# Norms by one-column sums, a power and a spreading product, with later deadlines for the recurrence and the heads

## The chip, the cores and the metric

The program runs on one core of a Trainium2 chip. The metric is the device time of one execution in microseconds. A core has five engines that run their own queues of instructions: TensorE (PE in the profile; PEld is its weight load, which can run beside a product), VectorE (DVE), ScalarE (ACT), GpSimd (POOL) and SyncE (SP, which here issues the DMA transfers). Semaphores tie the queues together; within one queue instructions start in order.

## The reference

A residual block over 2048 tokens of 1024 features, in fp32. RMS norms stand in five places of it: before the input projection, on the recurrent branch, before the feed-forward part and at the end (the retention heads have a norm of their own, per head).

```python
def rms_norm(x, gain):
    xf = x.astype(jnp.float32)
    y = xf * lax.rsqrt(jnp.mean(xf * xf, axis=-1, keepdims=True) + NORM_EPS)
    return (y * gain.astype(jnp.float32)).astype(x.dtype)
...
    u = rms_norm(h, norm1_gain[l])
    proj = u @ w_in[l].astype(dt)
    x_lru, g_lru, q, k, v, g_ret = jnp.split(proj, SPLITS, axis=-1)
    xc = causal_depthwise_conv(x_lru, lru_conv_w[l], lru_conv_b[l])
    hl = rg_lru(xc, ...)
    y_lru = rms_norm(hl.astype(dt) * jax.nn.gelu(g_lru), lru_norm_gain[l])
    o = head_group_norm(retention_chunkwise(qh, kh, vh), ret_norm_gain[l])
    y_ret = o.reshape(bsz, slen, D_RET) * jax.nn.silu(g_ret)
    h = h + jnp.concatenate([y_lru, y_ret], axis=-1) @ w_out[l].astype(dt)
    u = rms_norm(h, norm2_gain[l])
    up = causal_depthwise_conv(u @ ffn_up_w[l].astype(dt), ffn_conv_w[l], ffn_conv_b[l])
    a_branch, v_branch = jnp.split(up, 2, axis=-1)
    h = h + (jax.nn.gelu(a_branch) * v_branch) @ ffn_down_w[l].astype(dt)
return rms_norm(h, final_norm_gain)
```

## The kernel before

Activations lie transposed: features on the 128 partitions, tokens in columns, two groups of 1024 tokens (g is 0 or 1). [...]

**Products.** A projection works on blocks in a Strassen scheme: a unit of seven block products (`px`, `pe`, `py` and `pq` are their PSUM banks) makes what eight plain ones would. Each fp32 product is made of three of a reduced type: a block is cast into a high part (ACT, `wh` for weights and `bh` for activations), the rest is subtracted (DVE, `wl` and `bl`), and PE runs high by high, high by low and low by high. So a block product is twelve PE instructions 128x512 between whose operands ACT and DVE stand. `wv` is a half block of that kind, `s` a sum of two weight blocks `wa` and `wb`. There are 745 block products in the program: the input projection for both groups (A0, A1: products 0 to 171), the output projection (B0, B1), the up projection (24 units per group) and the down projection. Product numbers below count them in PE's order.

**Norms.** Where a norm is due (class `SumSq` and function `rstd`), ACT squares each 128x1024 tile, DVE adds the squares into `sqacc`, PE multiplies a half of `sqacc` by a matrix of ones (`mst`: every partition gets the sum), ACT takes the root of it with the mean and epsilon folded in, and DVE takes the reciprocal into `rb`, which `normed` multiplies in. That is done by the recurrence's norm (`LruGroup`), the norm behind the output projection (`NormGroup`) and the last one (`FinalGroup`; its `piece` does the last 1024 columns in pieces of 512, 256 and 256). Norm 1 sums over tokens on partitions instead: there the sums are a column `ms`, POOL raises it to the power -0.5 (`cst`), `diagonal` makes diagonal blocks `dg` of it on DVE, and PE spreads them over partitions with the matrix of ones (`pb`), which ACT copies into `rb`.

**What sets the order.** A planner (class `Flow`) emits all instructions, engine by engine, in the order in which they come in its own planned time. Pieces of work are generators; `yield t0 + 8` gives the rest of a piece the due tick `t0 + 8`, and a tick is one block product. Among instructions that could start, the one with the earliest due tick goes first. The planner's costs are methods `cost_pe`, `cost_v`, `cost_a` and `cost_p`. `LruOut` is the recurrence of one 128-feature tile: `first` makes convolution, gates (`pa`, `pg`), exponent, root and scan, `second` the gelu gate. `QkOut` and `VgOut` do rotation, transposes (`pt`), scores (`sc`) and outputs (`po`) of a head. Tiles come from 54 slots in SBUF; PSUM has three banks of the kind `sm` for all small products. The trace counts each product of fp32 operands (`mst`, `pb`, `pt`) as two PE instructions, the planner's order as one.

Every instruction of the program is recorded under one line of the source, that of the helper that calls the engine (L122), so the trace is read by tiles.

Of the kernel before, what the change touches and what calls it, by code (L numbers as in the profile page):

```python
# [25 lines left out]
F32 = mybir.dt.float32  # L26
# [22 lines left out]
SOON = 1.5  # L49
ISSUE = 0.45  # L50
# [50 lines left out]
class Engine:  # L101
# [30 lines left out]
    def cost_v(self, op, n, args, kw):  # L132
        if op == "tensor_tensor_scan":
            return 0.2 + 2.1e-3 * n
        if op in ("tensor_scalar", "tensor_copy", "memset"):
            return 0.15 + 0.535e-3 * n
        if op == "bn_stats":
            return 0.3
# [175 lines left out]
def hymba_block_kernel(ctx: ExitStack, tc: tile.TileContext, xh, xn, win, wout, wup, down, gates, vecs,  # L314
# [100 lines left out]
    eps = cp.tile([P, 1], F32, name="eps")  # L415
# [21 lines left out]
    def constants():  # L437
        yield v.memset(cst, -0.5)
        yield v.memset(eps, EPS)
# [119 lines left out]
    class Unit:  # L559
# [13 lines left out]
        def weights(self, t0):  # L573
# [3 lines left out]
            def first():  # L577
# [5 lines left out]
                fl.spawn(sums(), t0 - 5)  # L583
                yield t0 - 6
# [3 lines left out]
            def sums():  # L588
# [4 lines left out]
                yield t0 - 4  # L593
                self.w["s1"] = yield from split(s1, "w")
                self.there["s1"].on = True
                yield t0 - 2
# [7 lines left out]
                yield t0 + 2  # L604
# [7 lines left out]
            fl.spawn(first(), t0 - 8)  # L612
# [345 lines left out]
    def diagonal(rt, n):  # L958
        dg = yield Slot("dg")
        op = None  # L960
        for t in range(n):
            o = v.tensor_scalar(out=blk(dg, t), in0=idt, scalar1=rt[:, t:t + 1], scalar2=None, op0=ALU.mult)
            op = op + o if op else o
        yield op
        return dg

    def spread(rt, out):

        yield have["idt"]
        dg = yield from diagonal(rt, NCH)  # L970
        r = yield Slot("rb")
        for n in range(2):
            pb = yield Bank("sm", "pb")
            op = None
            for t in range(4):
                o = pe.matmul(blk(pb, t), ones, blk(dg, 4 * n + t), start=True, stop=True)
                op = op + o if op else o
            yield op
            yield a.copy(r[:, half(n)], pb)
            free(pb)  # L980
        free(dg)
        out.append(r)

    def rstd(ss, n, out):

        r = yield Slot("rb")
        for i in range(2):
            pm = yield Bank("sm", "mst")
            yield pe.matmul(pm, ones, ss.acc[:, half(i)], start=True, stop=True)
            yield a.activation(r[:, half(i)], pm, AF.Sqrt, scale=1.0 / n, bias=eps)  # L990
            free(pm)
            yield v.reciprocal(r[:, half(i)], r[:, half(i)])
        free(ss.acc)
        out.append(r)
# [31 lines left out]
    def norm1(g, start, due):  # L1026
# [4 lines left out]
        def one(t):  # L1031
# [6 lines left out]
            if left[0] == 0:  # L1038
                yield v.tensor_scalar(out=ms, in0=ms, scalar1=1.0 / D, scalar2=EPS, op0=ALU.mult, op1=ALU.add)
                yield p.tensor_tensor(out=ms, in0=ms, in1=cst.to_broadcast([P, NCH]), op=ALU.pow)  # L1040
                out = []
                yield from spread(ms, out)
                rb1[g] = out[0]
# [5 lines left out]
    class LruOut(PlainOut):  # L1049
# [6 lines left out]
        def second(self):  # L1056
            t0 = self.unit.t0
            yield t0 + 12
# [578 lines left out]
```

## Time and profile before

| | us |
|---|---|
| median of 3 runs | 2222.85 (2222.07 to 2223.22) |
| the profiled execution | 2223.36 |
| its span in the profile | 2221.6 |
| PE busy | 2165.6 |
| DVE busy | 1805.9 |
| ACT busy | 1237.3 |
| POOL busy | 25.9 |

Busy times are sums over the whole span; what an engine did in one stage is read from the trace in order of time. An idle time in brackets behind a PE instruction is time in which PE had nothing to run, and the name behind the arrow is the instruction that ended last of those that it waited for.

### The profile page before, as it was taken

To read this page: it belongs to the slowest core of one execution; us is meant where nothing else is said; L and a number is where in the kernel's file an instruction comes from. 1 tells how busy PE (TensorE), PEld (TensorE's weight loads), DVE (VectorE), ACT (ScalarE), POOL (GpSimd) and SP (SyncE) were. 2 spreads that over 40 slices of the span, in tenths; PEclk is the share of its full clock that TensorE was granted. 3 is DMA by queue.
4 is the path that set the end of the run, shared out by engine and by line. 5 is a ranking of instruction groups with operands and counts; after the bars stand their busy time and mean duration, and the time that the engine had idled before them with its cause. 6 is when DMAs were issued, how large, how long until landed. Compare 5 with 4: busy or idle time off the path is not lost.

```text
span 2221.6 us, 26370 instructions
## 1 busy us (share of the span) xinstructions
PE 2165.6 (97%) x9772; PEld 1776.6 (80%) x9772; DVE 1805.9 (81%) x2250; ACT 1237.3 (56%) x1773; POOL 25.9 (1%) x22
## 2 busy tenths in 40 slices
PE   9989989999999999999999999999999999999996
PEld 7868867888788887888888878888888788878885
DVE  7999788777675788989788897878788887798776
ACT  6665565556633166666666866666667444344341
POOL 0000000000000000000000000000000000000000
PEclk9999999999999999999999999999999999999998
DMA  8965355133656953444233532323236577589762
GB/s 324 372 212 200 111 201 166 60 96 116 207 183 236 330 214 127 175 139 173 93 105 128 209 118 83 122 90 114 90 108 227 225 283 288 220 304 344 256 226 76
DMA packets 140528, 408.32 MB, mean 184 GB/s; under 512 B 15728, under 2 KB 20208, under 8 KB 140400
## 3 DMA queue, kind: packets, MB, share of 16 engines
q1 hardware_dynamic: 140400, 406.65, 51.7%
q8 instruction: 76, 1.25, 0.2%
q14 instruction: 52, 0.43, 0.1%
HBM read 273.16 MB, written 125.04 MB: 179 GB/s over the span
## 4 chain that ended last, share of the span: by engine, by line
PE 89%; DVE 6%; ACT 2%; DMA 1%; issue 1%; SPq 0%; DVEq 0%; ACTq 0%
PE py L122 32%; PE px L122 21%; PE pe L122 20%; PE pq L122 12%; PE po L122 1%; DVE rb L122 1%; DVE res L122 1%; DVE o L122 1%; PE pk L122 1%; PE sc L122 1%; DVE bl L122 1%; PE pt L122 1%; DVE wl L122 1%; PE pa L122 1%; PE pg L122 0%
## 5 line engine op out<-in xcount | busy, mean ns | idle before, releaser
L122 PE MATMUL py<-bh,wh 128*128 128x512 f32 x728 | 289.9, 398 | 12.8 <-ACT wh L122 8.8
L122 PE MATMUL py<-bh,wl 128*128 128x512 f32 x728 | 287.8, 395 | 9.0 <-DVE wl L122 9.0
L122 PE MATMUL pe<-bh,wh 128*128 128x512 f32 x728 | 287.4, 395 | 1.6 <-DVE o L122 1.6
L122 PE MATMUL py<-bl,wh 128*128 128x512 f32 x728 | 286.7, 394 | 0.0
L122 PE MATMUL pe<-bl,wh 128*128 128x512 f32 x728 | 283.7, 390 | 2.2 <-DVE bl L122 2.1
L122 PE MATMUL px<-bh,wh 128*128 128x512 f32 x728 | 285.3, 392 | 0.0
L122 PE MATMUL pe<-bh,wl 128*128 128x512 f32 x728 | 283.6, 390 | 0.1
L122 PE MATMUL px<-bh,wl 128*128 128x512 f32 x728 | 283.5, 389 | 0.0
L122 PE MATMUL px<-bl,wh 128*128 128x512 f32 x728 | 283.3, 389 | 0.0
L122 ACT CAST wh<-s 128x1024 fp32r<-128x1024 f32 x182 | 190.4, 1046 | 162.9 <-DVE s L122 151.5
L122 DVE TENSOR_TENSOR wl<-s,wh 128x1024 fp32r<-128x1024 f32 x182 | 222.1, 1220 | 67.6 <-ACT wh L122 67.2
L122 DVE SCALAR_TENSOR_TENSOR c<-o,vec,c 128x1022 f32<-128x1022 f32 x192 | 245.3, 1279 | 13.8 <-ACT c L122 8.3
L122 PE MATMUL py<-bh,wv 128*128 128x512 f32 x728 | 242.5, 394 | 2.4 <-ACT o L122 1.6
L122 ACT COPY o<-py 128x512 f32<-128x512 f32 x204 | 119.9, 588 | 206.0 <-PE py L122 205.3
L122 ACT CAST bh<-raw 128x1024 fp32r<-128x1024 f32 x158 | 162.6, 1050 | 58.0 <-DMA raw<-g 15.0
L122 DVE TENSOR_TENSOR bl<-raw,bh 128x1024 fp32r<-128x1024 f32 x158 | 189.1, 1218 | 3.6 <-ACT bh L122 2.5
L122 PEld LDWEIGHTS py<-bh,wh 128*128 128x128 f32 x728 | 139.3, 191 | 44.9 <-ACT wh L122 10.9
L122 ACT ACTIVATE c<-o,vec 128x1024 f32<-128x1024 f32 x96 | 119.6, 1246 | 97.3 <-DVE o L122 95.9
L122 PEld LDWEIGHTS py<-bh,wl 128*128 128x128 f32 x728 | 138.7, 191 | 41.3 <-DVE wl L122 12.2
L122 PE MATMUL pq<-bh,wh 128*128 128x512 f32 (+1 forms) x432 | 168.5, 390 | 1.2 <-ACT bh L122 0.7
L122 PE MATMUL pq<-bl,wh 128*128 128x512 f32 (+1 forms) x432 | 165.2, 382 | 0.7 <-DVE bl L122 0.7
L122 PE MATMUL pq<-bh,wl 128*128 128x512 f32 (+1 forms) x432 | 165.0, 382 | 0.5 <-DVE wl L122 0.5
(136 smaller groups left out, 3822.5 us busy)
## 6 DMA issues: line engine op xcount, KB each, us to landing
wa<-in_dram SPq DMA_DIRECT2D x91, 512.0 KB, 4.0
wb<-in_dram SPq DMA_DIRECT2D x91, 512.0 KB, 4.8
h<-res SPq DMA_DIRECT2D x56, 512.0 KB, 3.5
g_T<-t SPq DMA_DIRECT2D x96, 256.0 KB, 2.4
raw<-g_T SPq DMA_DIRECT2D x48, 512.0 KB, 6.6
res<-h SPq DMA_DIRECT2D x48, 512.0 KB, 6.3
g<-c SPq DMA_DIRECT2D x76, 256.0 KB, 3.1
raw<-g SPq DMA_DIRECT2D x38, 512.0 KB, 6.7
```

The lines of the kernel that those rows point to most:

```text
L122: return Op(self.name, lambda: fn(*args, **kw), us, writes, reads, func=func)
```

## The change

`rstd` no longer multiplies by a matrix of ones. Each 128-column block of `sqacc` becomes the weights of a product with one column of ones, so that eight products leave the sums as a column of eight values per partition; DVE scales them and adds epsilon, POOL raises them to the power -0.5, and `spread` makes from each column a repeated column as weights, by which the identity is multiplied; ACT copies the two banks into `rb`. Norm 1 uses the same `spread` and loses its diagonal blocks. The planner gets a cost for reciprocals, of which a small one is left. `CH` puts off the due ticks of the recurrence and of the heads by 6; `WB`, for the weights, is 0.

```diff
+WB = 0
+CH = 6
...
+        if op == "reciprocal":
+            return 0.15 + 6.1e-3 * n
...
-        yield v.memset(eps, EPS)
...
-    def diagonal(rt, n):
-        dg = yield Slot("dg")
+    def spread(rt, c0, c1, r):
+
+        yield have["idt"]
+        for b in range(c0, c1, Q):
+            w = min(Q, c1 - b)
+            pb = yield Bank("sm", "pb")
+            op = None
+            for t in range(w // P):
+                k = (b - c0) // P + t
+                o = pe.matmul(blk(pb, t), rt[:, k:k + 1].to_broadcast([P, P]), idt, start=True, stop=True)
+                op = op + o if op else o
+            yield op
+            yield a.copy(r[:, b - c0:b - c0 + w], pb[:, 0:w])
+            free(pb)
+
+    def rstd(acc, n, r, c0=0, c1=HT):
+
+        nb = (c1 - c0) // P
+        rt = sp.tile([P, NCH], F32, tag="ms", name="ms")[:, 0:nb]
+        pm = yield Bank("sm", "mst")
         op = None
-        for t in range(n):
-            o = v.tensor_scalar(out=blk(dg, t), in0=idt, scalar1=rt[:, t:t + 1], scalar2=None, op0=ALU.mult)
+        for t in range(nb):
+            o = pe.matmul(pm[:, t:t + 1], acc[:, c0 + t * P:c0 + (t + 1) * P], ones[:, 0:1], start=True, stop=True)
             op = op + o if op else o
         yield op
-        return dg
-
-    def spread(rt, out):
-
-        yield have["idt"]
-        dg = yield from diagonal(rt, NCH)
-        r = yield Slot("rb")
-        for n in range(2):
-            pb = yield Bank("sm", "pb")
-            op = None
-            for t in range(4):
-                o = pe.matmul(blk(pb, t), ones, blk(dg, 4 * n + t), start=True, stop=True)
-                op = op + o if op else o
-            yield op
-            yield a.copy(r[:, half(n)], pb)
-            free(pb)
-        free(dg)
-        out.append(r)
-
-    def rstd(ss, n, out):
-
-        r = yield Slot("rb")
-        for i in range(2):
-            pm = yield Bank("sm", "mst")
-            yield pe.matmul(pm, ones, ss.acc[:, half(i)], start=True, stop=True)
-            yield a.activation(r[:, half(i)], pm, AF.Sqrt, scale=1.0 / n, bias=eps)
-            free(pm)
-            yield v.reciprocal(r[:, half(i)], r[:, half(i)])
-        free(ss.acc)
-        out.append(r)
+        yield v.tensor_scalar(out=rt, in0=pm[:, 0:nb], scalar1=1.0 / n, scalar2=EPS, op0=ALU.mult, op1=ALU.add)
+        free(pm)
+        yield p.tensor_tensor(out=rt, in0=rt, in1=cst.to_broadcast([P, nb]), op=ALU.pow)
+        yield from spread(rt, c0, c1, r)
...
-                out = []
-                yield from spread(ms, out)
-                rb1[g] = out[0]
+                r = rb1[g] = yield Slot("rb")
+                yield from spread(ms, 0, HT, r)
                 rb_there[g].on = True
...
         def second(self):
             t0 = self.unit.t0
-            yield t0 + 12
+            yield t0 + 12 + CH
             g = self.t2
             yield a.activation(g, g, AF.Gelu_apprx_tanh)
             yield self.scanned
-            yield t0 + 15
+            yield t0 + 15 + CH
             yield v.tensor_tensor(out=self.xc, in0=self.xc, in1=g, op=ALU.mult)
             free(g)
...
-            yield t0 + 7
+            yield t0 + 7 + CH
...
-            yield t0 + 8
+            yield t0 + 8 + CH
...
-            yield t0 + 10
+            yield t0 + 10 + CH
...
             if self.ss.left == 0:
-                out = []
-                yield from rstd(self.ss, 512, out)
+                r = yield Slot("rb")
+                yield from rstd(self.ss.acc, 512, r)
+                free(self.ss.acc)
                 left = [4]
                 for i in range(4):
-                    fl.spawn(self.normed(i, out[0], left), fl.tick + 6 + i)
+                    fl.spawn(self.normed(i, r, left), fl.tick + 6 + i)
...
-            yield self.unit.t0 + 8
+            yield self.unit.t0 + 8 + CH
             yield from self.head.rotate("q", self.t1)
 
         def second(self):
             hd, t0 = self.head, self.unit.t0
-            yield t0 + 12
+            yield t0 + 12 + CH
             yield from hd.rotate("k", self.t2)
-            yield t0 + 13
+            yield t0 + 13 + CH
             yield from hd.token_major(self.t2, "kT")
             hd.there["kT"].on = True
-            yield t0 + 14
+            yield t0 + 14 + CH
             yield from hd.scores()
...
-            yield t0 + 8
+            yield t0 + 8 + CH
...
-            yield t0 + 10
+            yield t0 + 10 + CH
...
-            yield t0 + 12
+            yield t0 + 12 + CH
             yield from hd.output(t0 + 14)
...
-            yield self.unit.t0 + 13
+            yield self.unit.t0 + 13 + CH
...
-                pm = yield Bank("sm", "mst")
-                yield pe.matmul(pm[:, 0:c1 - c0], ones, acc, start=True, stop=True)
                 r = yield Slot("rb")
                 r = r[:, 0:c1 - c0]
-                yield a.activation(r, pm[:, 0:c1 - c0], AF.Sqrt, scale=1.0 / D, bias=eps)
-                yield v.reciprocal(r, r)
+                yield from rstd(self.ss.acc, D, r, c0, c1)
```

Three places show how this moves instructions. The first is DVE in the first final norm (group 0 behind the down projection); `mst` and `ms` are that norm's sums, `h` the tiles it multiplies, `s_15449` (before) and `s_15493` (after) the sum of weight blocks of the next unit, `res` the down projection's results. Before:

```order
L122 RECIPROCAL rb<-rb 128x512
L122 TENSOR_TENSOR res<-res,py 128x512
L122 TENSOR_TENSOR wl<-s_15449,wh 128x1024
L122 RECIPROCAL rb<-rb 128x512
L122 TENSOR_TENSOR res<-res,pe 128x512
L122 TENSOR_TENSOR bl<-raw,bh 128x1024 x2
L122 TENSOR_TENSOR s_15449<-s_15449,wa 128x512
L122 TENSOR_TENSOR res<-res,py 128x512
L122 SCALAR_TENSOR_TENSOR h<-h,vec,rb 128x1024 x2
L122 TENSOR_TENSOR s_15449<-wa,s_15449 128x512
L122 SCALAR_TENSOR_TENSOR h<-h,vec,rb 128x1024 x2
L122 TENSOR_TENSOR wl<-s_15449,wh 128x1024
```

and after:

```order
L124 TENSOR_SCALAR ms<-mst 128x8
L124 TENSOR_TENSOR s_15493<-wa,wb 128x512
L124 TENSOR_TENSOR bl<-raw,bh 128x1024 x2
L124 TENSOR_TENSOR res<-res,py 128x512
L124 TENSOR_TENSOR wl<-s_15493,wh 128x1024
L124 TENSOR_TENSOR res<-res,pe 128x512
L124 TENSOR_TENSOR bl<-raw,bh 128x1024
L124 TENSOR_TENSOR s_15493<-s_15493,wa 128x512
L124 TENSOR_TENSOR s_15493<-wa,s_15493 128x512
L124 TENSOR_TENSOR wl<-wa,wh 128x1024
L124 TENSOR_TENSOR s_15624<-wb 128x512
```

The two RECIPROCALs are gone, a TENSOR_SCALAR stands in front instead, and the sums of weights and their `wl` stand ahead of the products with `h`, which follow further down.

The second is PE at the recurrence's norm of group 0, in the input projection, where `sqacc` are its sums and `py` the block product under way. Before, one of its two column sums and what follows on it:

```order
L122 MATMUL pe<-bh,wh 128x512
L122 MATMUL pe<-bl,wh 128x512
L122 MATMUL pe<-bh,wl 128x512
L122 MATMUL mst<-sqacc,ones 128x512
L122 MATMUL pt<-idt,o_2576 128x128 x8
L122 MATMUL sc<-o_2527,o_2576 128x128 x4
```

and after, the sums with the end of the product ahead of them and the start of the one behind:

```order
L124 MATMUL px<-bl,wh 128x512
L124 MATMUL px<-bh,wl 128x512
L124 MATMUL mst<-ones,sqacc 128x1 x8
L124 MATMUL py<-bh,wh 128x512
L124 MATMUL py<-bl,wh 128x512
```

and, twelve rows of `py` behind the sums, the first half of the spread:

```order
L124 MATMUL py<-bl,wh 128x512
L124 MATMUL py<-bh,wl 128x512
L124 MATMUL pb<-idt,ms 128x128 x4
L124 MATMUL px<-bh,wh 128x512
L124 MATMUL px<-bl,wh 128x512
```

Between the sums and the first spread stand the twelve instructions of one block product, and the second spread follows one product later.

The third is DVE at the recurrence in the input projection of group 1, from the root behind the exponent (`tt`) to the first `wl` behind the scan; `xc<-ea,hlast,gi` is the scan, `o_...` are outputs of a unit being rotated. Before:

```order
L122 TENSOR_TENSOR s_3136<-s_3136,wa 128x512
L122 TENSOR_TENSOR s_3136<-wa,s_3136 128x512
L122 SCALAR_TENSOR_TENSOR tt<-ea,tt 128x1024
L122 TENSOR_TENSOR gi<-gi,tt 128x1024
L122 SCALAR_TENSOR_TENSOR xc<-ea,hlast,gi 128x1024
L122 COPY hlast<-xc 128x1
L122 TENSOR_TENSOR wl<-s_3136,wh 128x1024
L122 TENSOR_TENSOR o_3150<-o_3150,pe 128x512
L122 TENSOR_TENSOR wl<-wa,wh 128x1024
```

and after:

```order
L124 TENSOR_TENSOR s_3268<-wa,s_3268 128x512
L124 TENSOR_TENSOR o_3073<-o_3073,rope 128x1024
L124 TENSOR_TENSOR sw<-sw,rope 128x1024
L124 TENSOR_TENSOR o_3368<-o_3368,pe 128x512
L124 TENSOR_TENSOR o_3073<-o_3073,sw 128x1024
L124 SCALAR_TENSOR_TENSOR tt<-ea,tt 128x1024
L124 TENSOR_TENSOR gi<-gi,tt 128x1024
L124 SCALAR_TENSOR_TENSOR xc<-ea,hlast,gi 128x1024
L124 COPY hlast<-xc 128x1
L124 TENSOR_TENSOR wl<-s_3268,wh 128x1024
```

The scan of before stands ahead of the `wl` of products 104 and on, that of after, six products later, ahead of the `wl` of product 111.

## Rows read from the trace of the kernel before

**Rows 1.** From the profile's page, its head with the span, the busy time of each engine (its share of the span, x instructions), and, from part 4, the shares of the chain of work that ended last.

```profile
span 2221.6 us, 26370 instructions
...
PE 2165.6 (97%) x9772; PEld 1776.6 (80%) x9772; DVE 1805.9 (81%) x2250; ACT 1237.3 (56%) x1773; POOL 25.9 (1%) x22
...
PE 89%; DVE 6%; ACT 2%; DMA 1%; issue 1%; SPq 0%; DVEq 0%; ACTq 0%
```

**Rows 2.** The trace in order of time, engine PE, the instructions before which PE stood idle longest: start in us, us, what, and in brackets the idle time before it and what ended that.

```profile
134.15 0.80 PE L122 MATMUL py<-bh,wh 128*128 128x512 f32 x1 [3.42 <-ACT o L122]
...
323.27 1.97 PE L122 MATMUL pt<-idt,o 128*128 128x128 f32 x8 [5.12 <-DVE o L122]
...
382.70 0.76 PE L122 MATMUL py<-bh,wl 128*128 128x512 f32 x1 [4.08 <-DVE wl L122]
...
605.52 0.50 PE L122 MATMUL py<-bh,wv 128*128 128x512 f32 x1 [1.36 <-ACT o L122]
...
610.35 0.50 PE L122 MATMUL pe<-bh,wh 128*128 128x512 f32 x1 [0.95 <-DVE o L122]
...
615.83 0.66 PE L122 MATMUL pt<-idt,o 128*128 128x128 f32 x4 [1.59 <-DVE o L122]
...
1990.86 0.80 PE L122 MATMUL py<-bh,wh 128*128 128x512 f32 x1 [3.67 <-ACT wh L122]
...
1993.25 0.80 PE L122 MATMUL py<-bh,wl 128*128 128x512 f32 x1 [1.17 <-DVE wl L122]
```

**Rows 3.** The chain of work that ended last, in order of time, behind those idle times and (at 392.31) one undisturbed product: start in us, us, what, how many instructions.

```profile
134.15 4.35 PE py L122 x12
...
323.27 1.97 PE pt L122 x8
325.24 1.71 PE sc L122 x8
326.94 3.39 PE py L122 x12
...
372.90 1.15 ACT tt L122
...
382.70 4.15 PE py L122 x10
...
392.31 2.72 PE px L122 x12
...
1993.25 4.42 PE py L122 x10
```

**Rows 4.** Busy time of each engine in the stretch behind the longest idle time: the stretch, its length, PE, PEld, DVE, ACT and POOL (x instructions), then the granted TensorE clock as a share of full speed, the DMA share and GB/s.

```profile
321.30:328.20 6.90, 4.93 (x20) 4.64 (x21) 6.87 (x5) 2.90 (x4) 0.00 (x0) 0.51 0.02 7
```

**Rows 5.** Groups of instructions, shapes kept apart: engine, operation, out<-in, shape, xcount, then busy us in all, mean ns of one, and the engine's idle time just before them with what ended most of it.

```profile
L122 DVE RECIPROCAL rb<-rb 128x512 f32<-128x512 f32 x11 | 36.7, 3342 | 0.3 <-ACT rb L122 0.3
...
L122 POOL TENSOR_TENSOR rs<-rs,cst 128x4 f32<-128x4 f32 x16 | 21.5, 1346 | 588.1 <-DVE rs L122 588.1
...
L122 PEld LDWEIGHTS mst<-sqacc,ones 128*128 128x128 f32 x26 | 4.6, 188 | 5.3 <-DVE sqacc L122 4.5
...
L122 DVE RECIPROCAL rb<-rb 128x256 f32<-128x256 f32 x2 | 3.5, 1748 | 0.0
...
L122 DVE TENSOR_SCALAR ms<-ms 128x8 f32<-128x8 f32 x2 | 0.3, 164 | 5.6 <-ACT xt L122 5.6
```

**Rows 6.** The trace in order of time, engine PE, then its weight loads (PEld): the sixteen instructions of one pair of spread banks, a column-sum bank among products, and two weight loads with no product under way.

```profile
36.84 1.95 PE L122 MATMUL pb<-dg,ones 128*128 128x128 f32 x16
...
1974.85 1.02 PE L122 MATMUL mst<-sqacc,ones 128*128 128x512 f32 x2
...
1975.94 0.40 PE L122 MATMUL px<-bl,wh 128*128 128x512 f32 x1
...
312.53 0.30 PEld L122 LDWEIGHTS mst<-sqacc,ones 128*128 128x128 f32 x2 [0.79 <-DVE sqacc L122]
```

**Rows 7.** The trace in order of time, engine DVE, in front of the 5.12 us, the 4.08 us and the 3.67 us of PE's idle time.

```profile
316.40 3.35 DVE L122 RECIPROCAL rb<-rb 128x512 f32<-128x512 f32 x1
...
323.13 3.35 DVE L122 RECIPROCAL rb<-rb 128x512 f32<-128x512 f32 x1
...
378.98 2.35 DVE L122 TENSOR_TENSOR_SCAN xc<-ea,hlast,gi 128x1024 f32<-128x1024 f32 x1
...
381.43 1.22 DVE L122 TENSOR_TENSOR wl<-s,wh 128x1024 fp32r<-128x1024 f32 x1
...
1974.39 3.35 DVE L122 RECIPROCAL rb<-rb 128x512 f32<-128x512 f32 x1
...
1988.99 0.68 DVE L122 TENSOR_TENSOR s<-wa,s 128x512 f32<-128x512 f32 x1
```

**Rows 8.** The trace in order of time, engine POOL, then DVE in the same stretch.

```profile
107.44 1.01 POOL L122 TENSOR_TENSOR rs<-rs,cst 128x4 f32<-128x4 f32 x1 [73.68 <-DVE rs L122]
...
113.24 2.54 POOL L122 TENSOR_TENSOR ms<-ms,cst 128x8 f32<-128x8 f32 x1 [1.03 <-DVE ms L122]
...
107.59 1.22 DVE L122 TENSOR_TENSOR bl<-raw,bh 128x1024 fp32r<-128x1024 f32 x1
...
113.08 1.22 DVE L122 TENSOR_TENSOR bl<-raw,bh 128x1024 fp32r<-128x1024 f32 x1
```

**Rows 9.** The end of the trace in order of time, engine DVE: the last eight instructions of the program's arithmetic.

```profile
2214.72 3.26 DVE L122 SCALAR_TENSOR_TENSOR res<-res,vec,rb 128x256 f32<-128x256 f32 x8
```

More of the change, by code (lines that the diff above doesn't have):

```diff
@@ L414, in hymba_block_kernel @@
     cst = cp.tile([P, 1], F32, name="cst")
-    eps = cp.tile([P, 1], F32, name="eps")
     msk = cp.tile([P, P], F32, name="msk")
@@ L582, in first @@
                 yield dma(raw["b"], self.wsrc[1])
-                fl.spawn(sums(), t0 - 5)
-                yield t0 - 6
+                fl.spawn(sums(), t0 - 5 - WB)
+                yield t0 - 6 - WB
                 self.w["a"] = yield from split(raw["a"], "w")
@@ L592, in sums @@
                 yield sub(s1[:, Q:D], A[:, 0:Q], B[:, 0:Q])
-                yield t0 - 4
+                yield t0 - 4 - WB
                 self.w["s1"] = yield from split(s1, "w")
                 self.there["s1"].on = True
-                yield t0 - 2
+                yield t0 - 2 - WB
                 yield sub(s1[:, 0:Q], s1[:, 0:Q], A[:, 0:Q])
@@ L603, in sums @@
                 free(s1)
-                yield t0 + 2
+                yield t0 + 2 - WB
                 t = yield Slot("wv", F32R)
@@ L610, in sums @@
                 free(B)
-            fl.spawn(first(), t0 - 8)
+            fl.spawn(first(), t0 - 8 - WB)
         def slices(self, name):
@@ L1362, in add @@
                 yield fl.tick - 5 + self.late
-                out = []
-                yield from rstd(self.ss, D, out)
+                r = yield Slot("rb")
+                yield from rstd(self.ss.acc, D, r)
+                free(self.ss.acc)
                 left = [KT]
                 for q in range(KT // 2):
-                    fl.spawn(self.normed(q, out[0], left), fl.tick + 2 * q + self.late * (q + 1))
+                    fl.spawn(self.normed(q, r, left), fl.tick + 2 * q + self.late * (q + 1))
         def normed(self, q, r, left):
```

## The prediction

> **What bounds the kernel now.** The page's head comes first [rows 1]: PE is busy for 2165.6 of 2221.6 us, DVE for 81%, and PE holds 89% of the chain that ended last. So time saved on DVE or ACT is worth something only where PE stands idle for it. Next I read PE's idle times in order of time [rows 2]: they come in five short places. Their names used below: *d* (PE waits at 134.15), *a* (323.27), *b* (382.70), *c* (605.52 to 615.83), *g* (1990.86 and 1993.25). Then I read the chain behind them [rows 3], because an idle time costs more than its length: twelve instructions of a product take 2.72 us in the undisturbed row at 392.31, but 4.35 at 134.15; ten take 4.15 at 382.70 and 4.42 at 1993.25 (ten are worth 2.27). The granted clock of one such stretch is 0.51, the lower of the two levels, 1.2 GHz [rows 4], after PE had stood idle for 5.12 us. Last, DVE in front of these places [rows 7] tells what held it: RECIPROCALs of 3.35 us in *a* and *g* (and two more in *c*), the recurrence (a scan of 2.35 us) ahead of the `wl` that PE needs in *b*.
>
> **The change, part by part.** All sums are against the profiled execution: 2223.36 us, which is the span plus 1.76; it lies 0.5 above the median of 2222.85.
>
> *PE work.* Five norms of 1024 columns (two of the recurrence, two behind the output projection, one of the first final group) lose two column-sum products 128x512 and get eight 128x1 and eight 128x128. A column-sum bank takes (1975.94 − 1974.85) − 0.23 of the `px` within it = 0.86 us [rows 6], two are 1.72. A spreading product is two instructions, and sixteen start over 1.95 us with the last one's length of 0.28 in it: 0.11 each [rows 6], so eight products 1.78. The trace has no product of one column. From above: its weight load isn't hidden at all, 0.188 us [rows 5] x 16 = 3.0. From below: it costs almost nothing. The nearest row is a pair of weight loads with no product under way, 0.30 for two of 0.188, so 0.11 apart [rows 6]; I take 0.11 x 16 = 1.78. A norm then costs 3.56 for 1.72: +1.85, five norms **+9.3** (+0.3 with free one-column products, +15.3 at the upper end). The last group's pieces are counted at the tail. Norm 1 keeps its number of spreading products.
>
> *New wait.* In the norms of before PE is never needed after the column sum. Now the spreading products stand in PE's queue behind a power on POOL, and behind them the next product. Between the sums and the first spread PE has one product, 2.72 us (the last such norm of the two behind the output projection has ten). The chain beside it: TENSOR_SCALAR 0.164 [rows 5], behind whatever DVE is doing (up to 1.22), and the power. POOL's powers take 1.35 in the mean [rows 5]; 1.01 when the power began at 107.44, before DVE's subtraction of 107.59; but 2.54 when it began at 113.24, just behind the subtraction of 113.08 that ended at 114.30 [rows 8]. So the power waited for that subtraction. In the new order a subtraction stands right behind TENSOR_SCALAR on DVE, so the chain is 0.2 + up to 1.2 + 1.0 to 2.5, or 1.2 to 3.9 against 2.72: a wait of 0 to 1.2 at each of four norms. I take **+1.7** in all (bounds 0, and 12.5 if every one of five waits is fully open at 2.5).
> The Trainium skill, "SBUF — State Buffer", section "SBUF: two separate sides", says that a DVE instruction with two SBUF inputs and a GpSimd one that reads SBUF exclude each other for a whole instruction; the pair at 113 agrees (2.54 against 1.01). It also lets the lock go to whoever starts first, so a power could hold up DVE by its own length; no row of before shows that, and the sum would move by under 1.3 a norm.
>
> *DVE and ACT work removed.* Eleven RECIPROCALs of 3.34 and two of 1.75 [rows 5] are 40.3 us of DVE; Sqrt with its table goes from ACT. All of it that lies beside a busy PE is worth nothing. By place:
> - *g*, 3.67 + 1.17 idle and 4.42 − 2.27 = 2.15 at the lower clock: 7.0. The RECIPROCAL of 1974.39 and a second one hold DVE for 6.7, and `s`, from which PE's next weights come, is made only at 1988.99 [rows 7], while PE wants them at 1987.19. In the new order both `s` and the `wl` behind it stand ahead of the `h` products. I take **−6.0**; 0.9 is left for DVE being full there.
> - *c*, 1.36 + 0.95 + 1.59 = 3.9. Two RECIPROCALs of a full DVE go, and the deadlines move the head's rotations away: **−3.7**.
> - *b*, 4.08 and 4.15 − 2.27 = 1.9: 6.0. Here no RECIPROCAL stands; the deadlines alone act. In the new order the recurrence comes six products later and meets the next unit's `wl`, again directly behind its scan. In before its last part, from 372.90 to that `wl`'s end at 382.65, takes 9.75 us [rows 3, 7]. In the new order this part can start some 8.6 us behind the start of product 105 (my estimate from the same instructions: gates 5.6, a table load and an exponent 2.4, a copy 0.6), so that it ends at 18.3; PE needs the `wl` behind six products of 2.72 and some 2.6 of gate and transpose products, at 18.9. **−5.7**, the least certain term: one instruction more ahead of it and half the stall is back.
> - *a*, 5.12, and 2.4 at the lower clock (eight `pt` 1.97 for 1.06 at 0.11 each, twelve `py` 3.39 for 2.72, half of eight `sc`'s 1.71): 7.5. The RECIPROCALs of 316.40 and 323.13 go [rows 7], but the next ten products now have the recurrence beside them: by the instructions in the new order and their mean durations 39 us of DVE against 35 of PE (an estimate), and two table loads on ACT. The jam stays, shifted: **−1.7** (0 to −7.5).
> - *d*, 3.42 idle, 1.63 at the lower clock, and some shorter idle times behind it. The spread of the second norm 1 now stands directly behind product 33's small ones on PE, and behind ACT's last square and a power; by the rows that is a wait of about 5 in place of 3.42, with the shorter ones mostly gone: **−0.9** (−5 to +6).
>
> Together −18.0. The up and down projections up to the first final norm keep their order on every engine: nothing.
>
> *Tail.* Three RECIPROCALs (one of 3.34, two of 1.75 [rows 5]) lie on DVE's almost unbroken last 22 us, which end at 2217.98 [rows 9]. Without them 6.8 are free; but the last piece pays TENSOR_SCALAR, power, spread and copy with DVE idle, 2.0 to 3.5, the piece ahead of it much the same, and PE has 0.9 more before its last product. Between 1 us gained and 1 lost: **−0.5** (−2 to +2).
>
> Sum: 9.3 + 1.7 − 18.0 − 0.5 = −7.5, so 2215.9 for the profiled execution and **2215.4** beside the median. What this kernel's runs tell from no change is about 0.2%, 4.4 us.
>
> **The rivals.**
> 1. *One-column products are nearly free.* For it: the 128-wide ones start 0.11 apart for 128 columns, and the loads might hide behind the product ahead. Against it: two loads without a product are also 0.11 apart. It takes off up to 1.78 x 5 = 8.9: about 2207.5, with 1 left. The Trainium skill, "TensorE: Matmul & The Clock Gate", section "Back-to-back issue gap", gives about 25 ns as the floor of small products; by that 16 are an estimated 0.4 us a norm and the time is 2208.4; the section itself says that weight loads bind beside it, and no row here shows one column.
> 2. *The jam only moves.* DVE's and ACT's work in the first projection stays what it was but for the RECIPROCALs, and later deadlines merely push it on to the next unit. Then *a*, *b* and *d* come back elsewhere (+8.3) and the time is about 2223: no change. For it: in the new order the scan still stands directly ahead of a `wl` in *b*. Against it: DVE has 81% and slack behind each jam.
> 3. *Slower: PE waits for POOL.* One mechanism: the spread at the head of PE's queue, behind a power that itself waits for DVE. If the power comes 2.5 us after PE at five norms (+12.5 instead of 1.7) and norm 1's spread costs 6 more than before instead of 0.9 less, the time is 2215.4 + 10.8 + 6.9 = 2233. It decides once the waits and *d* together are 7.5 worse than I take them; at 0.6 a wait worse (+3.1) the gain is within 0.2% already. For it: 2.54 at 113.24, and the subtraction behind TENSOR_SCALAR. Against it: a product of 2.72 lies between.
>
> **How the numbers follow.** My sum 0.47, rival 1 0.16, rival 2 0.22, rival 3 0.15. The range: below, 2207 less some 3 for *a* or *d* coming out well, 2204; above, no change and half of rival 3, 2228. For the likeliest case alone 2210 to 2219. Faster by over 0.2% (below 2218.4): nearly all of the sum and rival 1, 0.61; within it 0.23 (rival 2 and the sum's edge); slower 0.16.
>
> **What would show it.** In the changed profile: no idle time over 1.5 us near 378 and 1987; the one near 318 still there in some form within the next ten products; the sixteen instructions of a norm's column sums 1.7 to 1.8 us of PE; the first `pb` of a norm with an idle time under 1.2 before it; norm 1's second `pb` with about 5. I am wrong if *b* or *g* stay, if the one-column products are far from 0.11 each, or if `pb` waits 2 us or more behind POOL at the five norms.

## The result and the profile after

The changed kernel takes 2207.18 us (median of 6 runs, 2206.14 to 2210.37), the kernel before, timed on the same chip in the same rounds, 2223.03: a ratio of 0.993 with a 95% interval of 0.9917 to 0.9943. Forecast were 2215.4 and a range of 2204 to 2228. So the sign was right and the time lies in the range, but the gain is 15.9 us where 7.4 were worked out. The profiled execution took 2206.14, its span is 17.2 shorter than before.

The page's head of the changed kernel, as [rows 1]:

```profile
span 2204.4 us, 26724 instructions
...
PE 2170.5 (98%) x9938; PEld 1793.2 (81%) x9938; DVE 1765.0 (80%) x2228; ACT 1224.0 (56%) x1763; POOL 42.0 (2%) x30
...
PE 93%; DVE 4%; DMA 1%; ACT 1%; issue 1%; POOL 0%; SPq 0%; POOLq 0%; DVEq 0%
```

PE is busy 5 us longer in a span that is 17 shorter: the gain lies in time in which it stood or was held up. In order of time, engine PE, the idle times of 1 us and more between 100 us and the up projection (start, length, what, and in brackets the idle time before it):

```profile
154.91 0.50 PE L124 MATMUL px<-bh,wl 128*128 128x512 f32 x1 [1.61 <-DVE wl L124]
...
169.24 0.50 PE L124 MATMUL py<-bh,wl 128*128 128x512 f32 x1 [2.78 <-DVE wl L124]
...
320.41 3.57 PE L124 MATMUL mst<-ones,sqacc 128*128 128x1 f32 x16 [3.04 <-DVE sqacc L124]
...
760.04 0.50 PE L124 MATMUL pq<-bh,wl 128*128 128x512 f32 x1 [1.46 <-DVE wl L124]
```

The last one is new and belongs to the norms: norms_only has it too (774.00, 1.46), the kernel before and deadlines_only don't. The one at 320.41 belongs to the deadlines: PE waits there for `sqacc`, and it does so for 3.03 in deadlines_only.

An idle time of the profile begins only at the modelled end of the record before, so short delays don't show in it. To set the two traces against each other I therefore take the time between the same block products (`px` 1 is the start of the first stretch of `px` products, and so on) and subtract PE's instructions there, each at the usual distance from its start to the next one's (0.227 us for 128x512, 0.428 for a column sum of that size, 0.111 for 128x128, 0.112 for one column). What is left is time lost, to waiting or to the lower clock, in us. The last two columns are two of the experiments below:

| place | between | before | changed | norms_only | deadlines_only |
|---|---|---|---|---|---|
| d | px 1 to 9 | 12.7 | 9.9 | 8.9 | 10.7 |
| | px 9 to 17 | 4.6 | 3.2 | 7.9 | 3.2 |
| a | px 17 to 21 | 9.8 | 7.0 | 2.8 | 10.4 |
| b | px 21 to 25 | 8.1 | 1.8 | 10.3 | 1.8 |
| | px 25 to 40 | 5.4 | 3.7 | 5.5 | 3.7 |
| c | px 40 to 48 | 6.8 | 4.0 | 7.7 | 3.2 |
| g | px 162 to 172 | 8.1 | 1.6 | 1.6 | 8.1 |

At the start of the up projection (px 48: 870.89 before, 861.34 after) the changed kernel is 9.55 ahead, behind the up projections and group 0's down projection, at the first final norm (px 162), 11.11, behind that norm (px 172) 15.79, at the end 17.2.

The new norms themselves. Groups of instructions of the changed kernel, columns as in [rows 5]:

```profile
L124 PE MATMUL pb<-idt,ms 128*128 128x128 f32 x128 | 18.0, 284 | 4.9 <-POOL ms L124 4.8
...
L124 POOL TENSOR_TENSOR ms<-ms,cst 128x8 f32<-128x8 f32 x7 | 14.6, 2082 | 1492.3 <-DVE ms L124 1492.3
...
L124 PE MATMUL mst<-ones,sqacc 128*128 128x1 f32 x96 | 13.0, 262 | 3.4 <-DVE sqacc L124 3.4
```

Of the RECIPROCALs one of four columns is left. In order of time, POOL's power and PE's instructions of three norms (the recurrence's of group 1, the one behind the output projection of group 0, the first final one), with what DVE runs beside the first two powers:

```profile
613.40 1.84 PE L124 MATMUL mst<-ones,sqacc 128*128 128x1 f32 x16
...
615.53 1.64 POOL L124 TENSOR_TENSOR ms<-ms,cst 128x8 f32<-128x8 f32 x1 [36.53 <-DVE ms L124]
...
615.96 2.35 DVE L124 TENSOR_TENSOR wl<-w,wh 128x1024 fp32r<-128x1024 f32 x2
...
617.97 1.05 PE L124 MATMUL pb<-idt,ms 128*128 128x128 f32 x8
...
707.02 1.22 DVE L124 TENSOR_TENSOR wl<-w,wh 128x1024 fp32r<-128x1024 f32 x1
...
707.18 2.55 POOL L124 TENSOR_TENSOR ms<-ms,cst 128x8 f32<-128x8 f32 x1 [58.48 <-DVE ms L124]
...
709.79 1.16 PE L124 MATMUL pb<-idt,ms 128*128 128x128 f32 x8
...
1962.25 2.02 POOL L124 TENSOR_TENSOR ms<-ms,cst 128x8 f32<-128x8 f32 x1 [1153.59 <-DVE ms L124]
...
1964.69 1.05 PE L124 MATMUL pb<-idt,ms 128*128 128x128 f32 x8
```

None of these `pb` has an idle time of PE in front of it: the power ends 0.80, 0.06 and 0.42 us ahead of it. The cover is one product, and it only just fits: at 709.79 the first `pb` starts 0.39 behind the product's last instruction, where 0.23 is usual, so that PE lost 0.16 there. Sixteen one-column instructions take 1.84, 0.115 each.

### The profile page after: what moved, and what is told of

Same layout as the page of the kernel before. It is cut to its first block, busy times and chain, and to the rows that moved or that the text cites. A ratio compares the mean times of both kernels' runs of the same rounds, so it can differ in the third digit from the quotient of the medians.

```text
span 2204.4 us, 26724 instructions
## 1 busy us (share of the span) xinstructions
PE 2170.5 (98%) x9938; PEld 1793.2 (81%) x9938; DVE 1765.0 (80%) x2228; ACT 1224.0 (56%) x1763; POOL 42.0 (2%) x30
## 4 chain that ended last, share of the span: by engine, by line
PE 93%; DVE 4%; DMA 1%; ACT 1%; issue 1%; POOL 0%; SPq 0%; POOLq 0%; DVEq 0%
PE py L124 33%; PE px L124 22%; PE pe L124 21%; PE pq L124 12%; PE po L124 1%; DMA raw<-in_dram 1%; PE sc L124 1%; PE pt L124 1%; PE pb L124 1%; PE pk L124 1%; PE pa L124 1%; PE pg L124 1%; DVE res L124 1%; PE mst L124 1%; DVE wl L124 0%
```

## The experiments

Twelve kernels were run. "Ahead" below is by how much the profiled execution starts a given `px` product earlier than the kernel before: it tells where a difference arises. The medians are set beside those of the kernel before in the same rounds (2223.0 to 2224.1).

**Taking the change apart.** Four kernels: the new norms alone, the deadlines alone, and each of before and deadlines with the planner's price of a RECIPROCAL put right.

norms_only, against the changed kernel:

```diff
-CH = 6
+CH = 0
```

deadlines_only, against the kernel before (the other twelve due ticks likewise):

```diff
+CH = 6
...
-            yield t0 + 7
+            yield t0 + 7 + CH
```

cost_only, against the kernel before, and deadlines_cost, against deadlines_only:

```diff
+        if op == "reciprocal":
+            return 0.15 + 6.1e-3 * n
```

> The new norms with the old deadlines (CH = 0). Theory 1, each part acts at its own places: PE pays about 1.85 more at each of five norms (+9.3); place g and the end still gain about 7 and 1.4, c and a half of what they gained (4), b and d stay as before: about 2219, 3 to 5 below the kernel before. Theory 2, the norms' form carries the whole gain and the deadlines little: 2207 to 2209.

> The old norms (root, RECIPROCAL) with the new deadlines (CH = 6). Theory 1: b goes (-6.4), d and a lose 3 each, c about half (-2), g and the end stay, PE pays nothing more: about 2209 to 2211. Theory 2: the deadlines alone change little, 2219 to 2224. Theory 3, the two need each other, since RECIPROCALs of 3.35 us meet the recurrence elsewhere: b goes but new idle times of 4 or more arise behind a RECIPROCAL, 2215 to 2219.

> The kernel before, with one number of the planner changed: a RECIPROCAL of 512 columns is planned with 3.3 us instead of 0.7 (the row says 3.34). Theory A, the old norm was slow because the planner put it ahead of the weights that PE waits for: g loses 5 or more of its 7 us, c and a 2 to 4, time 2212 to 2217. Theory B, DVE is simply full there and the RECIPROCALs have to be paid: within 3 us of the kernel before.

> Old norms, new deadlines, and the RECIPROCAL planned with 3.3 us. Theory A: what counts is where the planner puts things; without the 9.3 us of PE work of the new norms this is as fast as the whole change or faster, 2200 to 2207. Theory B: 40 us of RECIPROCAL on DVE can't be hidden in the input projection, 2210 or more.

| kernel | median, us | ratio to before, 95% interval | ahead at px 48 | at px 162 | at px 172 |
|---|---|---|---|---|---|
| changed | 2207.18 | 0.993, 0.9917 to 0.9943 | 9.6 | 11.1 | 15.8 |
| norms_only | 2222.72 | 0.9996, 0.9987 to 1.0005 | −4.4 | −4.9 | −0.2 |
| deadlines_only | 2208.69 | 0.9931, 0.9917 to 0.9944 | 14.5 | 14.6 | 14.7 |
| cost_only | 2227.56 | 1.0016, 1.0007 to 1.0025 | −5.3 | −5.1 | −3.4 |
| deadlines_cost | 2206.41 | 0.992, 0.9908 to 0.9933 | 16.7 | 16.9 | 17.1 |

The deadlines carry the gain: alone they give 14.4 of the 15.9 us, with every RECIPROCAL still on DVE. The norms alone change nothing that can be measured: they lose 4.4 in the projections, win 4.7 at place g, and 1.3 at the end (a span 1.1 shorter, from 0.2 behind). The two parts add: −4.4 + 14.5 = 10.1 ahead at px 48, where the changed kernel has 9.6. Theory 2 of the norms falls, and theory 1 was too kind to them in the projections: by the table they take 3.8 us off d and 7.0 off a, but 3.3 come back between the two, 2.2 at b and 0.9 at c, and PE has 7.4 more work. Theory 1 of the deadlines is near in time (0.3 below its range) and right on b; a, though, didn't lose 3 (9.8 became 10.4). In norms_only, engine PE at b:

```profile
379.89 0.79 PE L124 MATMUL py<-bh,wl 128*128 128x512 f32 x1 [5.45 <-DVE wl L124]
```

In deadlines_only little is left at b and c, and g stands untouched:

```profile
1976.23 0.79 PE L123 MATMUL py<-bh,wh 128*128 128x512 f32 x1 [3.68 <-ACT wh L123]
...
1978.63 0.80 PE L123 MATMUL py<-bh,wl 128*128 128x512 f32 x1 [1.18 <-DVE wl L123]
```

So b and c go with the deadlines, g with the norms, a with the norms too. The right price of a RECIPROCAL without the deadlines makes things worse: both theories fall there (B wanted it within 3 us of before, it is 4.5 above). The planner does move the RECIPROCALs, but one of them (320.08, 3.35 long) now stands on DVE ahead of the rotation that PE waits for at a, and the idle time there grows from 5.12 to 8.98 (cost_only, engine PE):

```profile
325.82 1.97 PE L122 MATMUL pt<-idt,o 128*128 128x128 f32 x8 [8.98 <-DVE o L122]
...
387.23 0.80 PE L122 MATMUL py<-bh,wl 128*128 128x512 f32 x1 [5.46 <-DVE wl L122]
```

With the deadlines it is worth 2.3 us, and old norms with the right price are as fast as the whole change. Theory B falls as well for deadlines_cost (2210 or more): most of the 40 us of RECIPROCAL can lie beside PE. Place g stays there as it was (8.0 of lost time).

**The recurrence or the heads.** Old norms; CH only in the class of the recurrence (lru_late), or only in the two of the heads (heads_late), at each of their due ticks. In lru_late, against the kernel before,

```diff
+CH = 6
...
     class LruOut(PlainOut):
...
-            yield t0 + 7
+            yield t0 + 7 + CH
```

and in heads_late

```diff
+CH = 6
...
     class QkOut(PlainOut):
...
-            yield self.unit.t0 + 8
+            yield self.unit.t0 + 8 + CH
```

> Old norms, only the recurrence's deadlines are put off by 6, the heads' stay. Theory R, the recurrence's scan ahead of a wl was what held PE: most of the 14 us come, 2209 to 2212, with b gone. Theory H, the heads' rotations and transposes were: within 4 us of the kernel before, with a and c as they were.

> Old norms, only the heads' deadlines are put off by 6. Theory R: b stays or grows, at most 4 us below the kernel before, 2219 to 2224. Theory H: a and c go, 2210 to 2214.

lru_late takes 2219.78 (0.9978, 0.9969 to 0.9987; 2.6 ahead at px 48), heads_late 2215.65 (0.9967, 0.9955 to 0.998; 6.3 ahead). Theory R falls: with the recurrence alone put off, 7.0 of the 8.1 lost at b remain, with the heads alone 3.8, with both 1.8. Theory H is nearer, but heads_late misses its range by 1.7 us. At px 48 the two parts sum to 8.8 of 14.5, in the medians to 11.7 (3.8 and 7.9) of 14.4, so that they help each other is seen in the profiles and isn't clear of the spread in the medians. Each leaves or makes a large idle time of its own. lru_late, then heads_late, engine PE:

```profile
171.09 0.79 PE L123 MATMUL py<-bh,wh 128*128 128x512 f32 x1 [8.26 <-ACT wh L123]
...
401.75 0.79 PE L123 MATMUL py<-bh,wl 128*128 128x512 f32 x1 [3.67 <-DVE wl L123]
```

```profile
135.41 0.50 PE L123 MATMUL py<-bl,wh 128*128 128x512 f32 x1 [3.46 <-DVE bl L123]
...
321.97 0.80 PE L123 MATMUL py<-bh,wh 128*128 128x512 f32 x1 [3.67 <-ACT wh L123]
```

With the recurrence alone put off, its `wl` jam isn't removed: it stands at 401.75 in place of 382.70, again behind the scan (DVE's scan ends at 400.37, the `wl` follows).

**Old norms where they cost nothing, new ones where they gain.** The deadlines and the old norms in the projections, the new form for the last norm's two groups. Against deadlines_only, with the change's `spread` and `rstd` beside the old ones as `spread2` and `rstd2`:

```diff
+                if self.vcol == V_NF:
+                    r = yield Slot("rb")
+                    yield from rstd2(self.ss.acc, D, r)
+                    free(self.ss.acc)
+                else:
+                    out = []
+                    yield from rstd(self.ss, D, out)
+                    r = out[0]
...
-                pm = yield Bank("sm", "mst")
-                yield pe.matmul(pm[:, 0:c1 - c0], ones, acc, start=True, stop=True)
                 r = yield Slot("rb")
                 r = r[:, 0:c1 - c0]
-                yield a.activation(r, pm[:, 0:c1 - c0], AF.Sqrt, scale=1.0 / D, bias=eps)
-                yield v.reciprocal(r, r)
+                yield from rstd2(self.ss.acc, D, r, c0, c1)
```

> The new deadlines; the old norms in the input and output projections, the new form only in the two last norms. Theory 1, the parts add by place: the products before the up projection come 14.5 earlier as with the deadlines alone, place g gives 5 to 6 net of its PE work, the end 1 to 1.5: 2201 to 2203. Theory 2, the new form's PE work in the projections was itself hidden in idle time and costs nothing: about 2207, as the whole change.

It takes 2202.56 (2200.80 to 2205.11), 0.9904 of before with 0.989 to 0.9917, and beats the changed kernel. Ahead at px 48 13.3, at px 172 19.5, at the end 20.8. Theory 1: the new form's PE work in the projections is paid, 7.4 us, of which the changed kernel gets about half back in lost time (place a has 11.2 here and 7.0 there).

**The price of PE's work and of the power.** In sums_twice each one-column product is issued twice and in power_long a second POOL instruction stands behind each power (a product with ones, which changes no value); both are planned at no cost, so the order is that of the changed kernel.

sums_twice:

```diff
             o = pe.matmul(pm[:, t:t + 1], acc[:, c0 + t * P:c0 + (t + 1) * P], ones[:, 0:1], start=True, stop=True)
+            o.calls = o.calls * 2
```

power_long:

```diff
-        yield p.tensor_tensor(out=rt, in0=rt, in1=cst.to_broadcast([P, nb]), op=ALU.pow)
+        o = p.tensor_tensor(out=rt, in0=rt, in1=cst.to_broadcast([P, nb]), op=ALU.pow)
+        o.calls += p.tensor_tensor(out=rt, in0=rt, in1=ones[:, 0:nb], op=ALU.mult).calls
+        yield o
```

> The changed kernel with every one-column sum issued twice, planned at no cost, so that the order is the same: 16 more PE instructions at each of five norms, 14 at the end of the program. Theory 1, PE's added work is paid in full, 0.11 an instruction: 1.8 a norm, 8.8 in all, and about 0.5 at the end: 2215 to 2217. Theory 2, in the projections it fills PE's idle time behind late operands, and only the norm in the down projection pays: 2 to 5 above the changed kernel, 2209 to 2212.

> The changed kernel with a second POOL instruction behind each power of the eight norms by column sums (a product with ones, which changes no value), planned at no cost, so that the order is the same. Theory 1, the one block product between the sums and the spread only just covers the power: each of four norms then waits 1 to 1.6, the end's two pieces each as much: 5 to 9 above the changed kernel. Theory 2, there is slack behind the power: within 3 of it, all of that at the end.

sums_twice takes 2224.47, the whole gain is gone (ratio to before 1.0002, 0.9992 to 1.0011). It lies above the ranges of both theories. Theory 1 is nearer, but 17 in the medians and 13.6 between the profiled executions are more than 80 instructions of 0.115 (9.2) and the 16 of the end. Most of the rest in the profile is clock. Stretches of sums_twice around the sums of the norm at 709.54 (length; PE, PEld, DVE, ACT, POOL busy; granted clock; DMA share; GB/s):

```profile
705.00:709.50 4.50, 4.50 (x21) 3.75 (x20) 1.23 (x1) 1.06 (x1) 0.00 (x0) 1.00 0.66 233
709.50:713.20 3.70, 3.70 (x34) 3.66 (x34) 0.69 (x1) 1.04 (x1) 0.00 (x0) 1.00 0.02 4
713.20:717.40 4.20, 4.20 (x12) 3.28 (x12) 1.30 (x2) 0.00 (x0) 2.55 (x1) 0.59 0.00 0
```

around those at 616.10, as many:

```profile
616.10:619.75 3.65, 3.65 (x34) 3.65 (x33) 0.07 (x1) 0.00 (x0) 0.00 (x0) 1.00 0.00 0
619.75:624.00 4.25, 4.25 (x25) 3.69 (x25) 4.24 (x6) 2.46 (x3) 1.64 (x1) 1.00 0.65 175
```

and of the changed kernel around the same sums as the first, half as many:

```profile
705.00:706.90 1.90, 1.90 (x18) 1.86 (x18) 0.69 (x1) 0.96 (x1) 0.00 (x0) 1.00 0.00 0
706.90:711.00 4.10, 4.10 (x22) 3.21 (x22) 1.31 (x2) 0.01 (x1) 2.55 (x1) 1.00 0.00 0
```

PE is busy throughout all three. Behind the 32 one-column instructions at 709.54 (3.63 us) the product that follows runs at 0.59, most of it at the lower level of 1.2 GHz, and so it does behind those at 805.45; behind those at 616.10 and 1971.06 the clock stays at 1.00. In the changed kernel it stays at 1.00 behind the sixteen at 613.40, 705.06, 797.80 and 1960.13. At a, where the clock is low already, the 32 take 6.99 where the sixteen took 3.57. By the measure of the table sums_twice loses 2.7 more at a and 2.9 more at c than the changed kernel, on top of 9.0 us of instructions up to the first final norm.

power_long takes 2209.74 (0.994, 0.9928 to 0.9953), 2.6 above the changed kernel. The test was weaker than planned: the added instruction took 0.2 to 1.1 us, not the 1.6 I had reckoned with. It shows all the same: the `pb` at 617.92 and 710.12 now have idle times of 0.30 and 0.28 in front of them and c loses 4.9 for 4.0, though px 48 comes only 0.3 later; the first final norm loses 0.6 more, the end 0.8 (idle times in front of `pb` of 1.03 and 4.17 for 0.76 and 3.66). Another 2.0 of the 3.5 between the profiled executions arise in the up projections, where there is no power. In time it is theory 2 (within 3), but not all of it comes at the end: there is little slack behind the power.

**Other deadlines.** The mixed kernel with CH of 3, 9 and 12.

```diff
-CH = 6
+CH = 3
```

> The mixed kernel with deadlines later by 3 in place of 6. Theory 1, the preparation of the next unit's weights wins over the recurrence and the heads as soon as their due ticks lie behind it, and 3 isn't enough: half of the 13 us of the projections is back, 2207 to 2211. Theory 2, any small shift does it: within 2 of the mixed kernel.

> The mixed kernel with deadlines later by 9. Theory 1: the gain is there already at 6, so within 3 of the mixed kernel, 2200 to 2206. Theory 2, the longer the better: 2195 to 2199. Theory 3, the late work meets the up projection's first units and holds them: 2207 or more.

> The mixed kernel with deadlines later by 12. Theory 1: as at 9, within 3 of the mixed kernel. Theory 2: below 2199. Theory 3: 2207 or more, with idle times of PE behind the last products of the input projection, where the output projection waits for the heads.

| CH | median, us | ratio to before, 95% interval | ahead at px 48 |
|---|---|---|---|
| 3 | 2222.64 | 0.9993, 0.9985 to 1.0002 | −5.4 |
| 6 | 2202.56 | 0.9904, 0.989 to 0.9917 | 13.3 |
| 9 | 2211.87 | 0.9947, 0.9935 to 0.996 | 0.6 |
| 12 | 2202.26 | 0.9907, 0.9894 to 0.9921 | 13.3 |

No theory holds for all three: not the threshold, not the longer the better, not the late end. 6 and 12 are equally good, 3 and 9 are not, and where PE waits is another place each time. The worst of CH 3, then one of CH 9, engine PE:

```profile
629.12 1.94 PE L123 MATMUL pt<-idt,o 128*128 128x128 f32 x8 [6.63 <-DVE o L123]
```

```profile
327.01 0.80 PE L123 MATMUL py<-bh,wh 128*128 128x512 f32 x1 [3.38 <-ACT o L123]
```

So the 6 isn't a law of this kernel but a good draw of the planner.

## Why the prediction was right or wrong

*The bound.* Right: what moved is PE's lost time, most of it in the five places. These aren't PE's only idle times of that size, as the forecast and [rows 2] have it: the kernel before has 1.76 and 1.13 at 1288.97 and 1290.83, 1.80 and 2.11 at 1749.83 and 1753.37, and 2.21 at 2206.47. The first four, in work that the change leaves in its order, are still there in the changed kernel.

*PE work, +9.3.* Right: 1.84 for sixteen one-column instructions at full clock, where 1.78 were taken; rival 1 (nearly free ones) is out, by sums_twice too. Not reckoned with: at 320.41 the sixteen stand behind an idle time of 3.04 and run at the lower clock, 3.57.

*New wait, +1.7.* Too much. At the five norms it is 0.16 in all, at 709.79; norm 1's spread of group 1 waits 0.42, where I had written 5. That a power waits for a subtraction stands, and the product of 2.72 nearly always covers it. My reading of its size was wrong, though: the 1.01 at 107.44 is a power over four columns, the 2.54 at 113.24 one over eight, and over eight it takes 1.64 where it doesn't wait (615.53). So of the 1.53 between those two rows 0.90 is the wait and 0.63 the columns. Rival 3 did not come.

*Place g, −6.0.* Right in cause and size: 8.1 of lost time (idle times of 4.84 and the lower clock behind them) became 1.6, so −6.5, and less the norm's 1.85 of PE work px 162 to 172 gain 4.7. It is the norms' doing: deadlines_only leaves it, norms_only takes it.

*Places b and c, −5.7 and −3.7.* Near in size: 8.1 became 1.8, 6.8 became 4.0. At c the cause was wrong: I gave it to the RECIPROCALs first, but deadlines_only, which keeps them, has 3.2 left, and norms_only 7.7. At b it is the deadlines, as I wrote, but not chiefly the recurrence's: put off alone they take 1.1 off b, the heads' alone 4.3.

*Places a and d, −1.7 and −0.9.* This is the step that failed in size: −2.7 and −2.8. "The jam stays, shifted" was too dark. At a the cause was as I put it, the RECIPROCALs: norms_only has 2.8 left, deadlines_only 10.4. (Of the two that I named the one of 323.13 can't have made the 5.12: it starts when the idle time ends.) Why the jam that I reckoned there, DVE's 39 us beside PE's 35, came out smaller is not shown; I take it that work with a later deadline could be late. At d the spread of the second norm 1 was to cost a wait of 5 and cost 0.42; either part alone takes 2 to 4 off. The deadlines left PE a wait and the lower clock in both places: behind 2.78 of idle time at 169.24 and behind 3.04 at 320.41. Engine PE's stretches of the changed kernel there, columns as in [rows 4]:

```profile
169.20:173.50 4.30, 4.26 (x12) 3.39 (x13) 4.27 (x5) 0.40 (x1) 0.00 (x0) 0.62 0.99 285
320.40:324.00 3.60, 3.59 (x17) 3.59 (x18) 2.23 (x2) 0.00 (x0) 0.00 (x0) 0.51 0.63 201
```

*What I had not priced.* Between the places, from px 9 to 17 and from 25 to 40, 10.0 us of lost time became 6.9, in pauses too short for the lists of idle times that I read. The deadlines do that.

*The whole projection part.* Against the span's 17.2 the forecast of 7.5 is short by 9.7: 6.4 in the projections, 1.6 in the up projections, 0.9 at g and 0.9 at the end. In my sum it came to −3.2 (stalls −12.0, PE work of four norms +7.4, waits +1.4); measured −9.55. Of the 6.4 missing, a and d make 2.9, the unpriced pauses 3.1, the waits 1.4; 0.3 at b and c and 0.8 more lost ahead of px 1 go off. So three terms missed to the same side, and the time still fell into the range because that was 24 us wide.

*Up projection, 0.* 1.6 ahead more, though PE's order is the same. Stretches of the same work in the kernel before, the changed one and the mixed one, columns as in [rows 4]:

```profile
1286.00:1298.00 12.00, 9.11 (x33) 6.81 (x32) 11.95 (x15) 5.80 (x10) 0.00 (x0) 0.86 0.59 218
```

```profile
1276.00:1288.00 12.00, 9.11 (x40) 6.90 (x39) 11.50 (x15) 6.61 (x11) 0.00 (x0) 1.00 0.62 218
```

```profile
1272.00:1284.00 12.00, 9.11 (x39) 6.93 (x38) 11.20 (x14) 6.91 (x11) 0.00 (x0) 1.00 0.58 215
```

The idle time is 2.89 in all three, the clock of the stretch 0.86 in one and 1.00 in two; deadlines_only and norms_only had it low again. Each kernel has one profile only, so whether that goes with the kernel or with the execution isn't shown. I take it for an accident and count it as luck: it is of a size with the spread of the runs.

*Tail, −0.5.* Right in sign: 1.4, within its bounds. At the end of the changed kernel no product covers the power, and PE stands idle for it (engine PE, and DVE and POOL ahead of the second):

```profile
2190.59 0.71 PE L124 MATMUL pb<-idt,ms 128*128 128x128 f32 x4 [0.76 <-POOL ms L124]
...
2191.75 3.26 DVE L124 SCALAR_TENSOR_TENSOR res<-res,vec,rb 128x256 f32<-128x256 f32 x8 [0.16 <-ACT rb L124]
2194.92 0.15 DVE L124 TENSOR_SCALAR ms<-mst 128x2 f32<-128x2 f32 x1
...
2195.15 0.70 POOL L124 TENSOR_TENSOR ms<-ms,cst 128x2 f32<-128x2 f32 x1 [4.61 <-DVE ms L124]
...
2195.90 1.22 PE L124 MATMUL pb<-idt,ms 128*128 128x128 f32 x4 [3.66 <-POOL ms L124]
```

POOL is named, but the power makes only 0.70 of the 3.66: the TENSOR_SCALAR ahead of it stands behind eight products of the piece before on DVE and begins 2.7 after the sums have ended (2192.25). Behind it DVE stands idle for 2.49 until the copy (2197.57), which is the 2.0 to 3.5 of the forecast.

*Rival 2, the jam only moves.* It didn't for CH 6. But it is what norms_only did in the projections (3.3 more lost between d and a, 2.2 at b), what lru_late did at b, and what CH 3 did. That DVE had slack, my point against it, doesn't decide it.

What stays open: why 6 and 12 fall well and 3 and 9 don't. That later deadlines let the next units' operands go first is a story that these four don't bear out. The forecast was read from the order with 6 as the planner gave it; that this order was a good one was luck.

## What to carry to other kernels

Where one engine is busy for 97% of the span, price an edit by the lost time of that engine, place by place, and take a change of two parts apart before believing what either does: here the norms' new form, which takes 40 us off DVE, made the projections 4 to 5 us slower and was worth 5 us at the one place behind them where RECIPROCALs stood in front of PE. Take each form where it gains: old norms where DVE has room, new ones where PE waits for them. And the parameters of a list scheduler are draws: try a few values before giving a reason for one.

## What the runs showed of the hardware

PE can be busy all the time in the profile while its clock falls, here with one-column products: behind 32 instructions of that kind in a row (3.63 us, no idle time on PE) the granted clock of the next 4.2 us was 0.59 at two norms (709.54 and 805.45 in sums_twice), while at two others (616.10 and 1971.06) it stayed at 1.00. Behind sixteen (1.84 us, at 705.06 in the changed kernel) it stayed at 1.00.

A power on POOL waits for a DVE instruction with two SBUF operands that is running when it begins, and not for one that begins later. Over eight columns it took 1.64 us at 615.53, although a `wl` subtraction began on DVE at 615.96, and 2.55 at 707.18, where such a subtraction was running since 707.02. The Trainium skill, "SBUF — State Buffer", section "SBUF: two separate sides", says that two such instructions shut each other out for a whole instruction, whichever starts first. The power at 707.18 agrees. The other way round the numbers differ: the subtractions that began while a power ran, at 615.96 here (two in 2.35) and at 107.59 in [rows 8] (1.22, a row that I had overlooked), took no longer than elsewhere, so that the power didn't hold DVE up. Over two columns the power took 0.70 (2195.15), so its length goes with the columns.
